# A chunked recurrence in one decoder trunk: three engines in a rewritten source order, the head norm in four stages, outputs in two tiles

## The chip, the cores and the metric

The kernel runs on 1 core of one Trainium2 chip. The metric is the device time of one execution in microseconds; a kernel's figure is the median of several runs. A run's time is a little longer than the span between its first and its last instruction in the trace.

## The reference, cut to what matters

The program is a two-layer decoder trunk over 512 tokens of width 1024: layer 0 is a sparse attention, layer 1 an RWKV-7 time mixing; each has a squared-ReLU MLP behind it. The change lies in the time mixing of layer 1, between the values and the output projection:

```python
def step(state, inp):
    r_t, w_t, k_t, v_t, kk_t, b_t = inp
    sa = jnp.einsum('bhvk,bhk->bhv', state, -kk_t)
    state = (state * w_t[:, :, None, :] + sa[..., None] * b_t[:, :, None, :]
             + v_t[..., None] * k_t[:, :, None, :])
    y = jnp.einsum('bhvk,bhk->bhv', state, r_t)
    return state, y
_, y = lax.scan(step, state0, (tm(rh), tm(wh), tm(kh), tm(vh), tm(kk), tm(bh)))
mean = jnp.mean(y, axis=-1, keepdims=True)
var = jnp.mean(jnp.square(y - mean), axis=-1, keepdims=True)
y = ((y - mean) * lax.rsqrt(var + LNX_EPS) * lnx_w + lnx_b)
bonus = jnp.sum(rh * kh * r_k, axis=-1, keepdims=True) * vh
out = (y + bonus).reshape(B, L, D) * g
return out @ w_o
```

There are 16 heads of 64 channels.

## The kernel before, in words

All of the time mixing stands in `rwkv()`. The scan over 512 tokens is done as 8 chunks of 64 tokens (NCH = 8). Within a chunk the recurrence is a triangular system: its 64x64 inverse is put together from two 32x32 diagonal inverses and an off-diagonal block. The diagonal inverses are made on VectorE by `invert()` and `solve()` (L999 to L1042) for four chunks at once: two halves, 0 for chunks 0 to 3 and 1 for chunks 4 to 7. One half is 30 pairs of a multiply (`pr`, L1025) and an add (`tn`, L1026) and a copy (L1029); then the tiles go to DRAM and back (`dm`, `dt`), to `T11` and `Mt`. `invert()` is a generator: `run(budget)` lets it go on by that many nanoseconds' worth of pairs, `until(f)` until half f is issued.

The values GEMM (L1203 to L1215) steps the generator with `run(RUNW)` in each of its 8 rounds. Its result is copied to `VT` by ScalarE (`vcopy`, L1223), and VectorE takes means over it (`vmean`, L1273). Before a chunk can start, its operands are made: `opl(n, j)` (j = 0, 1) has 32 small matmuls L1184/L1185 into a `d` bank, which VectorE masks into `abd` and `BL` (L1179, four instructions for each j); `opt(n)` (L1196) transposes eight blocks, copied out to `BL` (L1197, L1113 and, in part, L1111 on VectorE); `vload(n)` (L1280) adds the mean to v on GpSimd, into `sv`, and sends v to a `vb` tile with two DMAs. `merge1` (L1129) and `merge2` (L1139) make the off-diagonal block; between them stands a copy `sa`, behind them one into `Mt`.

A chunk's own chain on TensorE: `step_z` (L1308, z; reads `sv`, copied to `bd`), `step_u` (L1324, u; four copies L1113 into `sv`), `step_r` (L1317) and `step_y` (L1354) for the output, `step_s` (L1335) and `step_n` (L1342) for the next state, which VectorE scales into `sv` (L1346) and ScalarE copies into `bd` (L1348). So z of the next chunk waits for L1346. The output y is copied to a `y` tile (L1357).

`gnorm(n)` normalizes y over a head: square (ScalarE, L1378), sum (VectorE, L1379), root and two Newton steps (L234 to L239), scale (L1381), then on GpSimd the weight `lnw` (L1383), the bonus `bv` = `vb` times `bo` (L1386) and the sum (L1387). `turn(n)` (L1396) transposes y; `out(f)` (L1404) multiplies with the gate `gT` for the chunks of half f, and `wo(f)` (L1409) is the output projection, 8 groups of 24 matmuls of 128x256 over `oh`, `ol` and `w`, with high and low parts split on ScalarE (L93, L104), VectorE (L101) and GpSimd (L99). `g2` (L1244 to L1247, 8 groups of 4 matmuls of 128x512) makes the gate `gT`.

The order of the work: the loop over chunks stands in `manual_schedule` for TensorE alone, so TensorE runs in source order, and the scheduler places ScalarE's and VectorE's instructions by priorities. In the source the operands, the merge and the norm of neighbouring chunks are generators that are stepped between the three stages of a step; `fill()` puts `g2` groups (table G2P) and `wo(0)` groups (table WOP) at numbered places in between. `turn` stands two steps behind its chunk (TD = 2), `out(0)` in step 5, and four of the eight `wo(0)` groups in steps 6 and 7 (before y of chunk 7 is done), the other four behind it.

Of the kernel before, what the change touches and what calls it, by code (L numbers as in the profile page):

```python
# [765 lines left out]
def rwkv(c, x, ks, gi):  # L766
# [324 lines left out]
    bo = c.tmp.tile([128, NCH, 8], F32, name="bo", tag="bo", bufs=1)  # L1091
    for b in range(2):
        for s in range(2):
            nc.vector.tensor_copy(bo[E2[b], s::2].rearrange("p n (a e) -> p n a e", e=2), pbo[E2[s], :, :, b])
# [20 lines left out]
    def merge(n):  # L1115
        mt = Mt[n // 4][:, :, n % 4]
        t11 = T11[n // 4]
        with c.hp("merge"):
            sa = merge1(mt, t11, n)
        yield  # L1120
        with c.hp("merge"):
            merge2(mt, sa)
        yield

    def merge1(mt, t11, n):
# [9 lines left out]
    def merge2(mt, sa):  # L1135
# [57 lines left out]
    def opt(n):  # L1193
# [4 lines left out]
        for i in range(2):  # L1198
            cp(TE[i], BL[n][E2[1 - i], 1, :, 64:128], pt[E2[i], :, 1])
# [28 lines left out]
    for i in VL:  # L1228
        vcopy(i)
    del ps  # L1230
    SV, YY, gT = {}, {}, {}

    def g2():
        (ah, al), (bh, bl) = ((a.rearrange("p a b -> p (a b)") for a in c.wget(0)) for _ in range(2))
        nc.scalar.activation(bh[64:96], bl[64:96].bitcast(F32), AF.Copy)
        for m in range(KC):
            g2m(m, ah, al, bh)
            yield

    @c.site("g2")  # L1240
    def g2m(m, ah, al, bh):
# [4 lines left out]
        nc.tensor.matmul(p, al[:, ms], sg[0], start=False, stop=False)  # L1246
# [30 lines left out]
    def vload(n):  # L1277
# [4 lines left out]
        VB[n] = c.t("vb")  # L1282
        v4 = vt(n).rearrange("p (a b) e i -> p a b (e i)", b=2)
        for b in range(2):
            nc.sync.dma_start(VB[n][E2[b]].rearrange("p (a j) -> p a j", a=4), v4[:, :, b])

    w0 = None
    fill()
    vmean(0)
    vload(0)  # L1290
    for _ in opnd(1):
        fill()
    lnw = c.t("lnw").rearrange("p (q i) -> p q i", i=64)
    nc.sync.dma_start(lnw, c.aps["lnw"])
    bd = c.b8("bd", F32, (128, 2, 8, 2, 64))
    nc.gpsimd.memset(bd, 0.0)
    Zb, Sb = bd[:, 0], bd[:, 1]
    yT, o, xo = {}, {}, []

    @c.site("step_z")  # L1300
    def step_z(n):
        pz, py = c.bank("g", (128, 8, 64)), c.bank("g", (128, 4, 2, 64))
        if n == 0:
            for e in range(2):
                nc.gpsimd.memset(SV[n][E2[e], e], 0.0)
# [3 lines left out]
        cp(0, Zb[E2[0], :, 0], pz[E2[0]])  # L1309
        cp(ZE, Zb[E2[1], :, 1], pz[E2[1]])  # L1310
        return py

    @c.site("step_r")
    def step_r(n, py):
        if n:
            for q in range(8):
                nc.tensor.matmul(py[E2[q % 2], q // 2].rearrange("p a b -> p (a b)"), sl(AR, n, q)[:, 1],  # L1317
                                 Sb[:, q].rearrange("p a b -> p (a b)"), start=q < 2, stop=False, skip_group_check=True)

    @c.site("step_u")  # L1320
    def step_u(n):
# [4 lines left out]
        for b in range(2):  # L1326
            for e in range(2):
                cp(UE[2 * b + e], par(SV[n][:, e])[E2[e], :, b], pu[E2[b], :, e])
# [10 lines left out]
    def step_n(n, pn):  # L1339
# [11 lines left out]
    def step_y(n, py):  # L1351
# [265 lines left out]
```

## Time and profile before

| what | value |
|---|---|
| median of 3 runs | 1375.86 us (1373.76 to 1376.73) |
| the profiled execution | 1374.03 us |
| its span, first to last instruction | 1372.2 us |
| mean granted TensorE clock, share of full | 0.972 |
| busy: TensorE, VectorE, ScalarE, GpSimd | 94%, 58%, 43%, 12% of the span |
| last matmul of the values / first matmul of the MLP of layer 1 | 816.2 us / 1005.0 us |

The busy share of the whole span says little here: TensorE is full in the GEMMs around the recurrence. What the change touches is a stretch of some 170 us, and there the questions are which wait ends last at each step and which clock TensorE was granted. The profile gives the clock as a share: 1.00 is the full level (2.4 GHz), 0.50 the half level (1.2 GHz), and a stretch with 0.82 has had some of both.

### The profile page before, as it was taken

What the parts mean: (1) busy time and instruction counts of PE and PEld (TensorE: products, weight loads), DVE (VectorE), ACT (ScalarE), POOL (GpSimd) and SP (SyncE); (2) the same over time, 40 slices, a digit from 0 to 9 for tenths busy, and PEclk for the clock granted to TensorE, in tenths of its full rate; (3) what the DMA queues carried; (4) which work ended last, traced back from release to release, by engine and by line L of the source; (5) the groups of instructions that cost most, each with busy time, mean ns of one, the idle gap of its engine ahead of it and who ended that gap; (6) DMA issues with size and microseconds to landing.
All of it is one profiled execution on the core that took longest, in us unless ns stands there. A gap on an engine that the chain in (4) does not pass through costs nothing.

```text
span 1372.2 us, 20054 instructions
## 1 busy us (share of the span) xinstructions
PE 1295.9 (94%) x8197; PEld 1065.6 (78%) x8197; DVE 800.8 (58%) x1429; ACT 593.6 (43%) x1005; POOL 171.3 (12%) x168
## 2 busy tenths in 40 slices
PE   7989899999999999999999896877999999999997
PEld 6767566888888888898578674667988888888887
DVE  5689974553431445339888888577865532245422
ACT  5545693343311434228776332655543421134421
POOL 0386750000000000000000011334220000000000
PEclk9999999999999999999999895989999999999998
DMA  7100013221323224303302414433532222322401
GB/s 287 62 31 32 1 69 117 100 93 62 123 92 123 80 74 153 123 32 123 123 31 53 128 52 98 74 95 132 185 105 80 92 92 94 122 92 83 162 1 62
DMA packets 68283, 128.04 MB, mean 93 GB/s; under 512 B 32864, under 2 KB 39648, under 8 KB 67424
## 3 DMA queue, kind: packets, MB, share of 16 engines
q1 hardware_dynamic: 65952, 124.53, 27.7%
q10 hardware_dynamic: 2240, 2.24, 0.5%
q8 instruction: 64, 1.05, 0.3%
q14 instruction: 27, 0.22, 0.0%
HBM read 115.74 MB, written 6.82 MB: 89 GB/s over the span
## 4 chain that ended last, share of the span: by engine, by line
PE 80%; DVE 12%; issue 3%; ACT 2%; POOL 2%; DMA 1%; SPq 0%; ACTq 0%; DVEq 0%; POOLq 0%
PE g L119 20%; PE g L120 20%; PE g L121 20%; PE g L628 2%; PE d L613 1%; DVE rot L411 1%; DVE w L101 1%; DVE L L587 1%; DVE pr L1025 1%; DVE tn L1026 1%; POOL kl L99 1%; DVE acc L497 1%; PE g L1308 1%; PE g L993 1%; PE g L1324 1%
## 5 line engine op out<-in xcount | busy, mean ns | idle before, releaser
L101 DVE TENSOR_TENSOR w<-wraw,w 128x1024 fp32r<-128x1024 f32 x189 | 232.8, 1255 | 109.4 <-ACT w L93 109.1
L93 ACT ACTIVATE w<-wraw 128x1024 fp32r<-128x1024 f32 x198 | 201.2, 1048 | 139.9 <-DMA wraw<-in_wblk 106.9
L119 PE MATMUL g<-sh,w 128*128 128x512 f32 (+1 forms) x608 | 216.5, 356 | 0.0
L120 PE MATMUL g<-sl,w 128*128 128x512 f32 (+1 forms) x608 | 216.1, 355 | 0.0
L121 PE MATMUL g<-sh,w 128*128 128x512 f32 (+1 forms) x608 | 216.1, 355 | 0.0
L120 PE MATMUL g<-al,w 128*128 128x512 f32 x512 | 200.0, 391 | 0.2 <-DVE al L257 0.2
L119 PE MATMUL g<-ah,w 128*128 128x512 f32 x512 | 200.1, 391 | 0.0
L121 PE MATMUL g<-ah,w 128*128 128x512 f32 x512 | 199.9, 390 | 0.0
L273 ACT ACTIVATE sh<-r 128x512 fp32r<-128x512 f32 x64 | 40.4, 631 | 227.2 <-DVE r L271 227.2
L119 PEld LDWEIGHTS g<-sh,w 128*128 128x128 f32 x608 | 114.9, 189 | 16.4
L121 PEld LDWEIGHTS g<-sh,w 128*128 128x128 f32 x608 | 114.9, 189 | 16.3
L120 PEld LDWEIGHTS g<-sl,w 128*128 128x128 f32 x608 | 114.9, 189 | 16.2
L119 PEld LDWEIGHTS g<-ah,w 128*128 128x128 f32 x512 | 96.5, 189 | 20.2
L120 PEld LDWEIGHTS g<-al,w 128*128 128x128 f32 x512 | 96.4, 188 | 20.4 <-DVE al L257 0.6
L121 PEld LDWEIGHTS g<-ah,w 128*128 128x128 f32 x512 | 96.5, 189 | 20.1
L271 DVE SCALAR_TENSOR_TENSOR r<-g,rstd 128x512 f32<-128x512 f32 x64 | 44.1, 691 | 97.0 <-PE g L121 84.6
L275 DVE TENSOR_TENSOR sl<-q,sh 128x512 fp32r<-128x512 f32 x64 | 44.4, 693 | 75.1 <-ACT q L274 75.1
L295 DVE TENSOR_TENSOR x<-g,x 128x512 f32<-128x512 f32 x26 | 18.0, 691 | 107.4 <-PE g L121 107.4
L179 ACT ACTIVATE sq<-x 128x256 f32<-128x256 f32 (+1 forms) x56 | 26.7, 499 | 105.1 <-DVE x L295 56.4
L922 POOL MEMSET seg<- 128x512 f32 x1 | 0.5, 528 | 487.2 <-DVE xl L101 487.2
L597 ACT ACTIVATE L<-L,st 128x256 f32<-128x256 f32 (+3 forms) x64 | 35.1, 553 | 14.0 <-DVE st L595 13.9
L274 ACT ACTIVATE q<-r 128x512 f32<-128x512 f32 x64 | 39.4, 615 | 0.0
(310 smaller groups left out, 2458.6 us busy)
## 6 DMA issues: line engine op xcount, KB each, us to landing
wraw<-in_wblk SPq DMA_DIRECT2D x98, 1024.0 KB, 4.8
wraw<-in_wblk SPq DMA_DIRECT2D x5, 512.0 KB, 5.6
x<-in_xT SPq DMA_DIRECT2D x8, 256.0 KB, 5.1
x<-in_xT SPq DMA_DIRECT2D x2, 1024.0 KB, 6.5
xs<-x SPq DMA_DIRECT2D x2, 1024.0 KB, 4.9
abd<-AR SPq DMA_DIRECT2D x64, 32.0 KB, 1.9
vb<-VT SPq DMA_DIRECT2D x16, 128.0 KB, 3.8
x<-xs SPq DMA_DIRECT2D x2, 1024.0 KB, 5.1
```

The costliest lines, as they stand in the source:

```text
L93: s.wsp = s.nc.scalar.activation(hi, r, AF.Copy)
L101: s.nc.vector.tensor_sub(out, a, b)
L119: s.nc.tensor.matmul(p, whi[:, kc, :], ahi, start=first and kc == 0, stop=False)
L120: s.nc.tensor.matmul(p, whi[:, kc, :], alo, start=False, stop=False)
L121: s.nc.tensor.matmul(p, wlo[:, kc, :], ahi, start=False, stop=last and kc == KC - 1)
L179: nc.scalar.activation(sq, xk, AF.Square)
L271: nc.vector.scalar_tensor_tensor(r, p, 0.0, rstd, op0=OP.max, op1=OP.mult)
L273: nc.scalar.activation(hi, r, AF.Square)
L274: nc.scalar.activation(q, r, AF.Square)
L275: nc.vector.tensor_sub(lo, q, hi.bitcast(F32))
L597: nc.scalar.activation(L[g][:, :n], L[g][:, :n], AF.Exp, bias=nmx[:, g:g + 1], scale=0.125, accum_out=sm[:, g:g + 1])
L628: nc.tensor.matmul(po[HF[e]], v[sc // 2][:, j:j + 64], st8[tb, pr, e][:, sc], start=sc == 0, stop=sc == tb)
```

## The change

The loop over chunks becomes straight source order on three engines (`manual_schedule` for TensorE, ScalarE and VectorE), and all that the generators and `fill()` interleaved is written out:

- The inverse is finished first: `run(9e8)` and two `run(1)` stand ahead of the first `vcopy`. The later calls `run(RUN1)`, `run(RUN2)` remain in the source.
- All eight `g2` groups stand ahead of the first merge.
- A step n is z, `opl(n+1, 0)`, u, merge1 of chunk n+1, s, n, r, y, `opl(n+1, 1)`, merge2, opt, turn.
- `gnorm` is cut in four: `gA` (square), `gB` (sum), `gC` (root), `gD` (all the rest), placed in steps by the tables GA, GB, TU.
- `bo` is one copy; the bonus reads v straight from `VT`, so the 16 `vb` DMAs are gone. It is two GpSimd multiplies of 64 partitions instead of one of 128.
- y lies in two tiles of four chunks. The copies of z, u and sa are all on ScalarE.
- `out(0)`, the norms 6 and 7, turns 5 to 7 and all eight `wo(0)` groups stand behind the loop.

```diff
+    with c.tc.manual_schedule(engines=set(MAN)):
+        run(9e8)
+        run(1)
+        run(1)
+        for i in VL[:3]:
+            vcopy(i)
+        vmean(0)
+        vload(0)
+        opn(1, 0)
+        for i in VL[3:]:
+            vcopy(i)
+        opn(1, 1)
...
+        g2(0)
+        g2(1)
+        opt(1, (0, 0))
+        g2(2)
+        g2(3)
+        step_z(0)
+        for m in range(4, 8):
+            g2(m)
+        vload(1)
+        run(RUN1)
+        merge2(0, merge1(0))
+        for n in range(NCH):
...
+            if n:
+                step_z(n)
...
+            if n and more:
+                acopy(n + 1)
+                opn(n + 1, 0)
+                vload(n + 1)
+            for k in GB.get(n, ()):
+                gB(k)
...
+            step_u(n)
+            if more and n != 3:
+                sa[n + 1] = merge1(n + 1)
+            for k in GB.get(n, ()):
+                gC(k)
+            if more:
+                pn = step_s(n)
+                step_n(n, pn)
+            py = step_r(n)
+            if more:
+                sbd(n)
+            step_y(n, py)
+            for k in GB.get(n, ()):
+                gD(k)
...
+            if n and more:
+                opn(n + 1, 1)
+            if n == 3:
+                sa[4] = merge1(4)
+            if more:
+                merge2(n + 1, sa[n + 1])
+            if n and n < NCH - 2:
+                opt(n + 1, (0, 0) if n < 3 else TE)
+            for k in TU.get(n, ()):
+                turn(k)
+            for k in GA.get(n, ()):
+                gA(k)
+    c.prefetch(PFA)
+    out(0)
+    gB(6)
+    gC(6)
+    gD(6)
+    gA(7)
+    gB(7)
+    gC(7)
+    gD(7, nc.vector)
     w0 = wo(0)
...
+    turn(5)
+    turn(6)
+    for _ in w0:
+        pass
+    turn(7)
     out(1)
...
+MAN = (mybir.EngineType.PE, mybir.EngineType.Activation, mybir.EngineType.DVE)
+GA = {2: (0,), 3: (1, 2), 4: (3,), 5: (4,), 6: (5,), 7: (6,)}
+GB = {3: (0,), 4: (1, 2), 5: (3,), 6: (4,), 7: (5,)}
+TU = {4: (0,), 5: (1, 2), 6: (3,), 7: (4,)}
```

What this does to the order of an engine's instructions shows at three places. First VectorE around the end of the inverse's first half. Before, this stood there (L1179 are the masks of `opl(1, ...)`, L1273/L1274 is `vmean`, L1029 the copy that ends half 0):

```order
L1026 TENSOR_TENSOR tn<-tn,pr 128x5x26
L1179 TENSOR_TENSOR BL<-d,kon 128x4x64
L1025 TENSOR_TENSOR pr<-tn 128x108
L1179 TENSOR_TENSOR BL<-d,kon 128x4x64
L1026 TENSOR_TENSOR tn<-tn,pr 128x4x27
L1111 COPY BL<-d 64x8x64
L1025 TENSOR_TENSOR pr<-tn 128x84
L1274 TENSOR_SCALAR vm<-vm 128x16
L1273 TENSOR_REDUCE vm<-VT 128x16
```

Now the masks (L1171) and `vmean` (L1245) stand behind the last pair and the copy of half 1:

```order
L1025 TENSOR_TENSOR pr<-tn 128x30
L1026 TENSOR_TENSOR tn<-tn,pr 128x30
L1028 MEMSET tn 128x32
L1029 COPY tn<-tn 128x1024
L1245 TENSOR_REDUCE vm<-VT 128x16
L1246 TENSOR_SCALAR vm<-vm 128x16
L1171 TENSOR_TENSOR abd<-d,kon 64x4x64 x2
L1171 TENSOR_TENSOR BL<-d,kon 128x4x64 x2
L1171 TENSOR_TENSOR abd<-d,kon 64x4x64 x2
```

So `vmean`, the masks of chunk 1 and all that waits for them have moved from between the pairs of half 0 to behind the 30 pairs of half 1.

Second TensorE in step 6 before (L1342 is n, L1354 is y, L1396 a turn, L119 to L121 are `wo(0)`):

```order
L119 MATMUL g<-oh,w 128x256
L120 MATMUL g<-ol,w 128x256
L121 MATMUL g<-oh,w 128x256
L1342 MATMUL g<-sv,BL 64x64 x16
L1354 MATMUL g<-sv,BL 64x64 x16
L1396 MATMUL g<-ident,y 128x128 x4
```

And TensorE now from the end of step 6 on (L1131 is merge2, L1260 z, L1268 u, L1297 r, L1310 y, L1363 a turn):

```order
L1131 MATMUL g<-Mt,sa 32x32 x16
L1363 MATMUL g<-ident,y 128x128 x4
L1260 MATMUL g<-sv,abd 64x64 x16
L1268 MATMUL g<-bd,Mt 64x128 x8
L1297 MATMUL g<-bd,AR 64x128 x8
L1310 MATMUL g<-sv,BL 64x64 x16
L1363 MATMUL g<-ident,y 128x128 x12
L119 MATMUL g<-oh,w 128x256
L120 MATMUL g<-ol,w 128x256
```

The `wo(0)` matmuls have left the steps; the first of them stands behind three turns in a row, those of chunks 4, 5 and 6.

Third ScalarE at that place now (L1272 are the copies of u(7), L1315 y(7), L1364 a turn's copy, L1323 `gA`, L1335 `gC`, L93 and L104 high parts of `w` and of `ot`):

```order
L1272 ACTIVATE sv<-g 64x4x64 x4
L1335 ACTIVATE gst<-gst 128x8
L1315 ACTIVATE y<-g 128x512
L1364 ACTIVATE yT<-g 128x8x64
L1323 ACTIVATE sq<-y 128x512
L1364 ACTIVATE yT<-g 128x8x64
L1335 ACTIVATE gst<-gst 128x8
L93 ACTIVATE w<-wraw 128x1024 x4
L104 ACTIVATE oh<-ot 128x256 x6
L1323 ACTIVATE sq<-y 128x512
```

The norm of chunk 6 begins behind the copy of y(7), and the weights of `wo(0)` are split behind it; before, the first of these weights were split during steps 5 to 7.

## Rows read from the trace of the kernel before

**Rows 1.** Windows: length; busy PE, PEld, DVE, ACT, POOL; granted clock; DMA share, GB/s.
```profile
838.00:850.00 12.00, 7.83 (x112) 6.53 (x114) 10.99 (x32) 3.42 (x7) 0.00 (x0) 0.50 0.34 65
850.00:867.00 17.00, 16.79 (x372) 14.28 (x369) 10.59 (x30) 9.79 (x20) 3.32 (x4) 0.82 0.40 91
...
884.20:899.50 15.30, 11.42 (x274) 9.49 (x274) 9.09 (x19) 9.77 (x20) 5.03 (x5) 1.00 0.17 28
...
916.00:931.50 15.50, 12.10 (x271) 10.37 (x271) 13.33 (x24) 9.80 (x20) 5.78 (x5) 0.89 0.15 25
```

**Rows 2.** What TensorE waited for, 815 to 970 us: total us, times, longest.
```profile
PE g L1308 <- DVE sv L1346: 7.8, 7, 3.8
```

**Rows 3.** Timeline of TensorE, 815 to 854 us: start, us, instruction, idle before and releaser.
```profile
815.94 0.39 PE L1213 MATMUL g<-w,xh 128*128 128x512 f32 x1
816.16 0.39 PE L1214 MATMUL g<-w,xl 128*128 128x512 f32 x1
...
834.21 0.28 PE L1129 MATMUL g<-T,Mt 32*32 32x32 f32 x2 [9.04 <-DMA T<-dt]
...
851.61 2.40 PE L1342 MATMUL g<-sv,BL 128*64 128x64 f32 x31
```

**Rows 4.** VectorE by line, 810 to 828 us: count, busy us, mean ns, idle before.
```profile
L1273 DVE TENSOR_REDUCE vm<-VT 128x16 f32<-128x1024 f32 x4 | 4.8, 1212 | 3.3 <-ACT VT L1223 3.3
L1026 DVE TENSOR_TENSOR tn<-tn,pr 128x210 f32<-128x210 f32 (+9 forms) x10 | 2.8, 285 | 0.1
L1025 DVE TENSOR_TENSOR pr<-tn 128x198 f32<-128x198 f32 (+8 forms) x9 | 2.8, 316 | 0.2
...
L1179 DVE TENSOR_TENSOR BL<-d,kon 128x256 f32<-128x256 f32 x4 | 1.6, 409 | 0.0
```

**Rows 5.** VectorE by line, 828.8 to 851.6 us: all of half 1.
```profile
L1025 DVE TENSOR_TENSOR pr<-tn 128x30 f32<-128x30 f32 (+14 forms) x30 | 10.0, 332 | 1.0
L1026 DVE TENSOR_TENSOR tn<-tn,pr 128x30 f32<-128x30 f32 (+14 forms) x30 | 9.9, 331 | 1.0
L1029 DVE COPY tn<-tn 128x1024 f32<-128x1024 f32 x2 | 2.1, 1046 | 0.1
```

**Rows 6.** Timeline of ScalarE in chunk 3.
```profile
888.03 1.20 ACT L1113 ACTIVATE bd<-g 64x512 f32<-64x512 f32 x2
...
890.48 1.58 ACT L1113 ACTIVATE sv<-g 64x256 f32<-64x256 f32 x4 [0.47 <-PE g L1324]
893.86 0.63 ACT L1378 ACTIVATE sq<-y 128x512 f32<-128x512 f32 x1 [1.80 <-PE g L1139]
```

**Rows 7.** Timeline of TensorE, from z(7) to the first matmul of wo(1).
```profile
960.29 1.15 PE L1308 MATMUL g<-sv,abd 128*64 128x64 f32 x32
962.74 1.09 PE L1324 MATMUL g<-bd,Mt 128*64 128x128 f32 x16 [1.29 <-ACT bd L1113]
...
964.63 0.38 PE L119 MATMUL g<-oh,w 128*128 128x256 f32 x1
...
967.70 1.20 PE L1354 MATMUL g<-sv,BL 128*64 128x64 f32 x32
...
982.96 0.51 PE L119 MATMUL g<-oh,w 128*128 128x256 f32 x2
```

**Rows 8.** ScalarE and VectorE by line and form, 867 to 969 us: splitting w; scaling the state.
```profile
L93 ACT ACTIVATE w<-wraw 128x1024 fp32r<-128x1024 f32 x10 | 10.3, 1054 | 5.1 <-DMA wraw<-in_wblk 5.1
...
L1346 DVE TENSOR_TENSOR sv<-g,pc 64x512 f32<-64x512 f32 x11 | 7.6, 689 | 1.0 <-PE g L1342 0.7
```

**Rows 9.** Timeline of VectorE, 957 to 964 us: two low parts of w.
```profile
957.82 1.23 DVE L101 TENSOR_TENSOR w<-wraw,w 128x1024 fp32r<-128x1024 f32 x1 [0.84 <-ACT w L93]
...
961.13 2.24 DVE L101 TENSOR_TENSOR w<-wraw,w 128x1024 fp32r<-128x1024 f32 x1
```

**Rows 10.** Timeline of GpSimd, 938 to 965 us.
```profile
938.75 0.85 POOL L99 TENSOR_TENSOR ol<-ot,oh 128x256 fp32r<-128x256 f32 x1 [0.81 <-ACT oh L104]
...
961.02 1.26 POOL L1383 TENSOR_TENSOR y<-y,lnw 128x512 f32<-128x512 f32 x1 [6.18 <-DVE y L1381]
```

More of the change, by code (lines that the diff above doesn't have):

```diff
@@ L1113, in cp, with merge1 @@
             nc.scalar.activation(out, a, AF.Copy)
[L1115 to L1125, printed above, removed]
+    @c.site("merge")
+    def merge1(n):
+        mt, t11 = Mt[n // 4][:, :, n % 4], T11[n // 4]
         pa = c.bank("g", (128, 8, 64))[:, :, :32]
@@ L1133, in merge1, with merge2 @@
         return sa
-    def merge2(mt, sa):
+    @c.site("merge")
+    def merge2(n, sa):
+        mt = Mt[n // 4][:, :, n % 4]
         pm = c.bank("g", (128, 8, 64))[:, :, :32]
@@ L1308, in step_z @@
                 nc.tensor.matmul(pz[E2[e], q], AL[n][:, q, e], SV[n][:, e, q], start=True, stop=True)
[L1309 to L1318, printed above, removed]
+        for e in range(2):
+            nc.scalar.activation(Zb[E2[e], :, e], pz[E2[e]], AF.Copy)
     @c.site("step_u")
@@ L1346, in step_n, with step_r, sbd @@
             nc.vector.tensor_mul(SV[n + 1][E2[e], e], pn[E2[e]], pcb[E2[e]].to_broadcast([64, 8, 64]))
+    @c.site("step_r")
+    def step_r(n):
+        py = c.bank("g", (128, 4, 2, 64))
+        if n:
+            for q in range(8):
+                nc.tensor.matmul(py[E2[q % 2], q // 2].rearrange("p a b -> p (a b)"), sl(AR, n, q)[:, 1],
+                                 Sb[:, q].rearrange("p a b -> p (a b)"), start=q < 2, stop=False, skip_group_check=True)
+        return py
+    @c.site("step_r")
+    def sbd(n):
         for e in range(2):
@@ L1424, in wom @@
         nc.vector.tensor_add(xm, p, xm)
-    until(0)
-    w0 = wo(0)
-    for _ in merge(0):
-        fill()
-    with c.tc.manual_schedule(engines={mybir.EngineType.PE}):
-        for n in range(NCH):
-            if n == 3:
-                until(1)
-            s = step(n)
-            op, mg = iter(()), iter(())
-            if n + 1 < NCH:
-                if n % 2:
-                    vmean((n + 1) // 2)
-                vload(n + 1)
-                mg = merge(n + 1)
-                if n:
-                    op = opnd(n + 1)
-            for i in range(3):
-                next(s)
-                next(op, None)
-                if i < 2:
-                    next(mg, None)
-                if i == GN and n:
-                    gnorm(n - 1)
-                if i == TN and n >= TD:
-                    turn(n - TD)
-                    if n - TD == 3:
-                        out(0)
-                if 3 * n + i in PFS:
-                    c.prefetch(PFA)
-                if n < 3:
-                    run(RUN1)
-                fill()
@@ L1459, in rwkv, with opn @@
-    gnorm(NCH - 1)
-    for n in range(NCH - TD, NCH - 1):
-        turn(n)
-    pull(w0, 8)
-    turn(NCH - 1)
+    yT, o, xo, yq, sa = {}, {}, [], [], {}
+    def opn(n, j):
+        if j == 0:
+            BL[n] = c.b8("BL", F32, (128, 2, 8, 128))
+        opl(n, j)
+    with c.tc.manual_schedule(engines=set(MAN)):
[9 more added lines that the diff above has]
+            vcopy(i)
+        del ps
+        opn(1, 1)
+        (ah, al_), (bh, bl) = ((a.rearrange("p a b -> p (a b)") for a in c.wget(0)) for _ in range(2))
+        nc.scalar.activation(bh[64:96], bl[64:96].bitcast(F32), AF.Copy)
+        g2(0)
[10 more added lines that the diff above has]
+        for n in range(NCH):
+            more = n < NCH - 1
+            if n:
+                step_z(n)
+            if n % 2 and more:
+                vmean((n + 1) // 2)
+            if n == 1:
+                lnw = g3(c.t("lnw"))
+                nc.sync.dma_start(lnw, c.aps["lnw"])
+            if n and more:
[4 more added lines that the diff above has]
+                gB(k)
+            if n < 3:
+                run(RUN2)
+            step_u(n)
[12 more added lines that the diff above has]
+                gD(k)
+            if n < 2:
+                run(RUN2)
+            elif n == 2:
+                run(9e8)
+                run(1)
+                run(1)
+            if n and more:
[10 more added lines that the diff above has]
+                gA(k)
```

140 lines of the change are left out of this document (53 added, 87 removed).

## The prediction

> **What bounds the kernel now.** I read the windows first, then what TensorE waited for, then its timeline and that of the engines it waited for. Between the values GEMM and the first steps TensorE stands still or runs slowly: from 838 to 850 us it is busy 7.83 of 12 us at a granted clock of 0.50 (1.2 GHz), from 850 to 867 us it is full and the clock is 0.82 [rows 1]. The reader sees the cause in its timeline: behind the last value matmul at 816.2 it waits 9.04 us, up to 834.2, for the trip of the inverse through DRAM, and n(0) ends at 851.61 + 2.40 = 854.0 [rows 3]. In the loop a chunk is bound by hand-overs: from 884.2 to 899.5, 15.3 us at full clock, with one chunk in it and no other work, TensorE is busy 11.42, ScalarE 9.77, VectorE 9.09 [rows 1]; the wait that comes back in every chunk is that of z for the scaled state, 7.8 us over 7 times [rows 2]. Chunks with w splits beside them lose clock too (0.89 from 916 to 931.5) [rows 1]. In steps 6 and 7 `wo(0)` fills the gaps, so little is left behind y(7), which ends at 968.9; `wo(1)` starts at 982.96 [rows 7]. From there on both kernels do the same work, so I forecast when `wo(1)` starts.
>
> The sum is made against the profiled execution, 1374.0 us (span 1372.2 and 1.8 around it); the median of the runs, 1375.86, lies 1.8 above. A difference under 0.2%, about 2.7 us, can't be told from none here.
>
> **Part 1, the start: about 10 us later.** Ahead of `vmean` and the masks of chunk 1 VectorE now has the whole inverse. From 810.2 on: the rest of half 0, 2.8 + 2.8 us [rows 4], and a copy of 1.05 [rows 5], to 816.9. Half 1: 10.0 + 9.9 busy, 2.0 between them and a copy, 22.9 in all [rows 5], to 839.8. `vmean` 1.2 + 0.2 and four masks of 0.41 [rows 4]: 842.9. TensorE ends the values at 816.55 [rows 3] and has one half of `opl(1)` to do, about 1 us; the other half waits for the masks, since both `d` banks are taken. Everything in TensorE's source order stands behind it, g2 too. So it idles some 25 us, where it now idles in pieces.
>
> From 842.9 to the end of n(0), at full clock: half an `opl` 1.0; 8 g2 groups of 4 matmuls spaced 0.23 [rows 3], 7.3; opt 1.0; z 1.15, u 1.09 [rows 7]; n as long as z; the two merges 1.4 (my estimate from their 32 small matmuls each, under z's 32); the copies of sa and Mt, about 0.8 each, and of u, 1.58 [rows 6], in which TensorE waits; hand-overs 0.7. That is 18. Behind its idle time now, TensorE had 0.50 for 12 us and then 0.82 over 17 us, so about 6 us of those 17 at half [rows 1]; 6 us at half do 3 us of work, which puts n(0) at 864, against 854.0. Bounds: 861 (no clock loss) and 868 (half clock up to u). What covered the second half of the inverse before was TensorE's wait for the first; that cover is gone. The DMA trip of half 0 now lies inside the wait and costs nothing; that of half 1 is wanted only by chunk 4, some 40 us later. The `bo` copy, the memsets moved ahead and the 16 `vb` DMAs taken off SP's queue stand in nobody's wait: at nothing.
>
> **Part 2, the loop: about 27 us shorter.** A full chunk with norm and turn, from the end of n to the end of n. ScalarE sets the pace, since it is in order: scaled state 0.69 behind n [rows 8], its two copies and y 1.8, then what TensorE makes in the order r, y, opl, merge2 (3.9 behind n): Mt 0.8, two `BL` copies 1.2, the turn's copy 0.6, gA 0.63 [rows 6], which ends 7.4 behind n. z was ready at 6.75; its copies (1.20 [rows 6]) end at 8.6, u at 9.75, u's copies (1.58) at 11.3, n at 12.5. Without norm, turn and opt, n(1) follows in about 8.5; n(2) 11.4, n(3) 12.1; with two norms in a row and the late merge in it n(4) 14; n(5) and n(6) about 13.5 each. Sum 73. From n(6) to the end of y(7): scale 1.4, z 1.15, its copies 1.2, u 1.09, u's copies 1.58, y 1.2 [rows 6 to 8], with hand-overs 8. y(7) ends at 864 + 73 + 8 = 945. The clock: TensorE is busy nearly 11.4 of each 12.5, more than the 12.10 of 15.5 that had 0.89 [rows 1]; I take 4 to 8 us of loss, since there are gaps in each chunk, and y(7) at **951**, against 968.9 now. So the loop (from n(0)) takes 87 us, not 115. Of the 28 gained, four `wo(0)` groups (12) and the last g2 groups have only moved out.
>
> **Part 3, the tail: about 35 us longer.** Now 14.1 us lie between the end of y(7) and `wo(1)` [rows 7]. After: all eight `wo(0)` groups. One is 24 matmuls, 3.07 us from the first at 964.63 to y at 967.70 [rows 7]; eight: 24. But they cannot start at once. Both things they need begin behind y(7):
> - ScalarE, in order: copies of y, turn 4, square 6, turn 5, root 6, about 2.7; then four high parts of w at 1.05 [rows 8]: 6.9 behind y(7), and only then the high parts of the outputs.
> - VectorE, in order: norm 6 among eight products for the gate, about 8; then four low parts of w at 1.23, or 2.24 beside GpSimd [rows 9], 4.9 to 9.0; then a low part of an output. 13.3 to 17.5.
> - GpSimd, behind the norm's scaling at about 8: weight, low part, two bonus products, low part, sum, at 0.85 to 1.26 each [rows 10], 6.5 alone. turn(6), which stands ahead of the first `wo(0)` matmul, comes at 14.5, or 17 with delays.
>
> I take 16 us of idle time, midway, as both chains run beside each other. Behind it TensorE starts at half clock again, as at 838 [rows 1]: 3 us. `wo(0)` ends at 951 + 16 + 24 + 3 = 994. Then `wo(1)`: turn(7) has 23 matmuls (2.8 us) behind it as cover, but VectorE does eight products (3.5) and two w splits (2.5) before the first low part, and the copies ahead take 1.3: some 7.5 to 8 in a row, so a stall of 4 with bounds 0 and 6, and 1 for the clock. `wo(1)` starts at 999.5, against 982.96: **+16.5**, and 1374.0 + 16.5 is 1390.5; I say 1391.
>
> On the splits beside GpSimd the rows show 1.23 alone and 2.24 where GpSimd started an instruction 0.1 us earlier [rows 9, 10]. The Trainium skill ("SBUF — State Buffer", section Who interferes with whom) says that a VectorE instruction with two inputs in SBUF shares a port pair with GpSimd's reads, and that one of the two then blocks for the other's whole instruction. By that rule each of the four splits could wait out 1.26 us, 10.0 in all, and `wo(0)` would start 18 to 19 behind y(7), 1393; if GpSimd is the one that blocks, the turn is late instead. I keep 16, as the rows allow both 13 and 17.5.
>
> **The rivals.**
> 1. *The loop gains more than the tail loses: faster.* Place: ScalarE's queue in the loop. If its copies come early enough, TensorE paces a chunk with its own 11.2 (11.42 without the two starts of the next z [rows 1]) at full clock: n(6) at 864 + 8.5 + 5 x 11.2 = 928.5, y(7) at 936.5; the tail with the low ends (13 + 24 + 1.5 + 1) puts `wo(1)` at 976, 7 us earlier: 1367. It decides where y(7) ends before 943 with that tail, 12.5 for each of those five chunks. For it: ScalarE has under 9.8 of work per chunk [rows 1]; against: the square stands ahead of z's copies in its queue. With the tail as I forecast it, y(7) would have to end at 934.5, below that floor. 0.14.
> 2. *The two cancel:* y(7) at 943 to 946 with a tail of 39. 1372 to 1376. 0.07.
> 3. *The clock stays down:* the gaps of 1 to 2 us in each chunk and the idle 25 and 16 us keep it at about 0.8 over the loop and the start of `wo(0)`. 87 us with some 70 of TensorE work at 0.8 instead of 0.93: 10 to 12 more. 1402. For it: 0.82 over a window that was full [rows 1]; against: 1.00 in the chunk with 11.42 of 15.3 busy. 0.13.
> 4. *The change doesn't do what it says at the start:* the order of rows shows the inverse ahead, so only its price can be off. If VectorE does the pairs faster without interleaving (gaps of 2.0 gone), 2 us; this lies in the range.
>
> **How the numbers follow.** The forecast as told, 1383 to 1399, has 0.66. With rival 3 (0.13) slower cases hold 0.79; rival 2 0.07; rival 1 0.14. The range takes in the forecast, rival 2 and rival 3 up to 1402, leaving out rival 1 and the far end of 3: 1372 to 1402. Faster by over 0.2% 0.15, within 0.2% 0.07, slower 0.78.
>
> **What would show it.** Right: in the timeline of VectorE the masks of chunk 1 stand behind the copy of half 1 at about 841 to 843, and TensorE's longest wait, some 25 us, ends there with VectorE as releaser; n(0) ends near 864; z's follow each other in 12 to 14 us; y(7) near 951; then a second long wait of 13 to 18 us ending with a turn whose releaser is GpSimd's sum, or with the low part of `w`; clock near 0.5 behind both. Wrong: z's less than 11.5 apart from chunk 2 on, `wo(0)` starting under 10 us behind y(7), or TensorE at work between 820 and 840.

## The result, and the profile after

The changed kernel takes 1398.86 us, the median of 4 runs (1396.93 to 1400.9); the kernel before, in the same session, 1376.08 (1373.76 to 1376.73). The ratio is 1.0169, 95% interval 1.015 to 1.0188: **slower, by 22.8 us**, where +15 to +17 was forecast. It lies inside the range (1372 to 1402), near its upper end, and 0.1 us inside the 1383 to 1399 of the forecast as told. The profiled execution after has a span of 1397.7 us at a mean clock of 0.967, so 25.5 us more than the span of before; 2.0 of these stand ahead of the change already, since the values GEMM ends at 818.6 instead of 816.6.

What TensorE waited for, 815 to 1030 us after (total us, times, longest), four of the lines:

```profile
PE d L1176 <- DVE BL L1171: 25.0, 1, 25.0
...
PE g L1363 <- POOL y L1354: 19.3, 2, 16.2
...
PE g L1268 <- ACT bd L1262: 12.9, 7, 2.9
...
PE g L120 <- DVE ol L101: 4.5, 1, 4.5
```

The first line is the start (the second half of `opl(1)` for the masks), the second the tail (turns 5 and 6 for GpSimd's sum of the norm), the third the loop (u for the copies of z), the fourth the first low part of `wo(1)`. The wait of z for the scaled state [rows 2], 7.8 us before, is gone altogether.

The timeline of TensorE after, at the start and then from y(7) on (start, us, instruction, idle before and releaser), beside [rows 3, 7]:

```profile
844.57 0.44 PE L1176 MATMUL d<-AR,KB 64*64 64x128 f32 x1 [24.98 <-DVE BL L1171]
...
861.92 2.16 PE L1286 MATMUL g<-sv,BL 128*64 128x64 f32 x31
...
863.92 1.15 PE L1310 MATMUL g<-sv,BL 128*64 128x64 f32 x31
...
953.03 2.07 PE L1310 MATMUL g<-sv,BL 128*64 128x64 f32 x32
...
958.80 1.11 PE L1363 MATMUL g<-ident,y 128*128 128x128 f32 x4 [3.11 <-POOL y L1354]
...
976.10 1.12 PE L1363 MATMUL g<-ident,y 128*128 128x128 f32 x4 [16.18 <-POOL y L1354]
976.86 0.56 PE L119 MATMUL g<-oh,w 128*128 128x256 f32 x1
...
999.29 0.60 PE L1363 MATMUL g<-ident,y 128*128 128x128 f32 x4
...
1002.96 0.73 PE L119 MATMUL g<-oh,w 128*128 128x256 f32 x4 [0.32 <-ACT oh L104]
1008.22 0.58 PE L120 MATMUL g<-ol,w 128*128 128x256 f32 x1 [4.53 <-DVE ol L101]
```

n(0) ends at about 864, y(7) at 955.1, the first `wo(0)` matmul comes at 976.9, and `wo(1)` gets going at 1008.2 instead of 983. What ends the first wait is seen on VectorE, where the masks of chunk 1 come behind the copy of half 1 and `vmean`:

```profile
840.50 1.03 DVE L1029 COPY tn<-tn 128x1024 f32<-128x1024 f32 x1
...
842.90 0.86 DVE L1171 TENSOR_TENSOR abd<-d,kon 64x256 f32<-64x256 f32 x2
```

The windows after, beside [rows 1] (length; busy PE, PEld, DVE, ACT, POOL; clock; DMA share, GB/s):

```profile
838.00:850.00 12.00, 5.43 (x46) 4.53 (x47) 7.54 (x21) 1.05 (x2) 4.18 (x4) 0.56 0.40 98
850.00:867.00 17.00, 15.31 (x310) 12.52 (x312) 2.73 (x4) 12.34 (x26) 0.00 (x0) 1.00 0.21 33
900.00:917.00 17.00, 14.34 (x302) 11.80 (x303) 9.09 (x24) 9.26 (x22) 8.14 (x8) 0.80 0.11 18
...
960.00:980.00 20.00, 3.90 (x19) 3.91 (x20) 14.47 (x26) 10.46 (x20) 16.18 (x10) 0.50 0.37 141
```

In the last of these TensorE works 3.9 of 20 us, at the half level, while GpSimd is busy 16.18. That is the longest wait of the tail, and VectorE's and GpSimd's timelines show what stands in it:

```profile
963.16 4.62 DVE L101 TENSOR_TENSOR w<-wraw,w 128x1024 fp32r<-128x1024 f32 x4
967.71 1.09 DVE L101 TENSOR_TENSOR ol<-ot,oh 128x256 fp32r<-128x256 f32 x3
```

```profile
963.39 6.53 POOL L1353 TENSOR_TENSOR y<-y,lnw 128x512 f32<-128x512 f32 x1 [4.65 <-DVE y L1346]
969.88 0.90 POOL L99 TENSOR_TENSOR ol<-ot,oh 128x256 fp32r<-128x256 f32 x1
970.87 2.18 POOL L1351 TENSOR_TENSOR bv<-VT,bo 64x512 f32<-64x512 f32 x2
973.12 1.25 POOL L99 TENSOR_TENSOR ol<-ot,oh 128x256 fp32r<-128x256 f32 x1
974.34 1.70 POOL L1354 TENSOR_TENSOR y<-y,bv 128x512 f32<-128x512 f32 x1
```

The weight multiply of norm 6 takes 6.53 us where it took 1.26 [rows 10]. It begins 0.2 us behind the first of VectorE's four splits of w. These run undisturbed at 1.2 each, three low parts of outputs follow them without a gap, and the multiply ends 1.1 us behind the last of the seven, so it did nearly all of its 1.26 us of work behind them. All that turn(6) waits for queues behind it on GpSimd. In the kernel before the same two instructions met the other way round: the multiply began at 961.02, 0.1 us ahead of a split, took its 1.26, and the split took 2.24 instead of 1.23 [rows 9, 10].

### The profile page after: what moved, and what is told of

The parts are those of the page before. It is cut to its first block, busy times and chain, and to the rows that moved or that the text cites. A ratio compares the mean times of both kernels' runs of the same rounds, so it can differ in the third digit from the quotient of the medians.

```text
span 1397.7 us, 20048 instructions
## 1 busy us (share of the span) xinstructions
PE 1291.2 (92%) x8197; PEld 1061.7 (76%) x8197; DVE 793.3 (57%) x1407; ACT 601.2 (43%) x1024; POOL 182.9 (13%) x176
## 3 DMA queue, kind: packets, MB, share of 16 engines
q10 hardware_dynamic: 2240, 2.24, 0.5%
q8 instruction: 64, 1.05, 0.3%
## 4 chain that ended last, share of the span: by engine, by line
PE 81%; DVE 12%; ACT 3%; issue 2%; POOL 1%; DMA 0%; ACTq 0%; DVEq 0%; POOLq 0%
PE g L120 20%; PE g L119 20%; PE g L121 20%; PE g L628 2%; DVE w L101 1%; DVE rot L411 1%; DVE tn L1026 1%; DVE pr L1025 1%; PE d L613 1%; DVE acc L497 1%; DVE L L587 1%; DVE m L495 1%; PE g L1268 1%; PE g L1286 1%; ACT bd L1262 1%
## 5 line engine op out<-in xcount | busy, mean ns | idle before, releaser
L101 DVE TENSOR_TENSOR w<-wraw,w 128x1024 fp32r<-128x1024 f32 x189 | 229.0, 1238 | 108.7 <-ACT w L93 108.6
L93 ACT ACTIVATE w<-wraw 128x1024 fp32r<-128x1024 f32 x198 | 200.6, 1048 | 134.7 <-DMA wraw<-in_wblk 102.9
L119 PE MATMUL g<-sh,w 128*128 128x512 f32 (+1 forms) x608 | 216.5, 356 | 0.0
L121 PE MATMUL g<-sh,w 128*128 128x512 f32 (+1 forms) x608 | 216.1, 355 | 0.0
L119 PE MATMUL g<-ah,w 128*128 128x512 f32 x512 | 199.6, 390 | 0.0
L121 PE MATMUL g<-ah,w 128*128 128x512 f32 x512 | 199.2, 389 | 0.0
L119 PEld LDWEIGHTS g<-sh,w 128*128 128x128 f32 x608 | 114.9, 189 | 16.4
L121 PEld LDWEIGHTS g<-sh,w 128*128 128x128 f32 x608 | 114.9, 189 | 16.3
L120 PEld LDWEIGHTS g<-sl,w 128*128 128x128 f32 x608 | 114.9, 189 | 16.2
L121 PEld LDWEIGHTS g<-ah,w 128*128 128x128 f32 x512 | 96.1, 188 | 20.0
L119 PEld LDWEIGHTS g<-ah,w 128*128 128x128 f32 x512 | 96.1, 188 | 19.9
L120 PE MATMUL g<-ol,w 128*128 128x256 f32 x128 | 38.1, 299 | 4.5 <-DVE ol L101 4.5
L1176 PE MATMUL d<-AR,KB 64*64 64x128 f32 x256 | 18.7, 285 | 25.0 <-DVE BL L1171 25.0
```

What stands on the lines that cost most here:

```text
L93: s.wsp = s.nc.scalar.activation(hi, r, AF.Copy)
L101: s.nc.vector.tensor_sub(out, a, b)
L119: s.nc.tensor.matmul(p, whi[:, kc, :], ahi, start=first and kc == 0, stop=False)
L120: s.nc.tensor.matmul(p, whi[:, kc, :], alo, start=False, stop=False)
L121: s.nc.tensor.matmul(p, wlo[:, kc, :], ahi, start=False, stop=last and kc == KC - 1)
L1176: nc.tensor.matmul(pl[E2[1 - e], e, q].rearrange("p a t -> p (a t)"), k[:, 1], ar.rearrange("p a t -> p (a t)"), start=True, stop=True)
```

## The experiments

Each kernel is compared with the kernel before on the same chip, so what an edit is worth I take from the ratios: the changed kernel has 1.0169, and 0.001 is 1.4 us. Intervals are some 0.0025 to either side, so the difference of two ratios is known to some 3.5 to 5 us only: by time alone e1, e2, e3 and e4 can't be told from the changed kernel, and e13 hardly; there the traces have to carry the reading. Lines are numbered as in each kernel, up to seven away from one another. Positions in different traces differ through what comes ahead of the change (the values GEMM ends at 818.6 in the changed kernel and at 817.5 to 821.9 in the others), so I compare distances too, above all from the start of y(0) to that of y(7), "the loop": 113.9 us before, 89.1 after. e2 and e3 leave the loop as it is and have 88.0 and 89.6, e1 and e9 have 88.8 and 91.0; that is the scatter. Part of it is the clock: over the loop it was 0.94 on average in the changed kernel and in e2, and 0.91 in e9.

**1. The inverse interleaved again (e1, e9).**

```diff
-        run(9e8)
-        run(1)
-        run(1)
         for i in VL[:3]:
             vcopy(i)
```

> The changed kernel without the three calls that finish the inverse ahead of vmean; the later calls run(9000) and run(2500) then have pairs to place. My theory (the 30 pairs of half 1 on VectorE are what TensorE's 25.0 us wait for the masks consists of): that wait falls to under 5 us, n(0) ends near 842 instead of 864, and the kernel takes 1377 to 1383 us instead of 1399. Rival (the pairs are work that VectorE has to do somewhere before chunk 4, so the loop pays them back): n(0) earlier, but z(4) at most 8 us earlier, 1391 to 1396.

Measured: 1393.89 us, ratio 1.0151 (1.0125 to 1.0176). y(0) starts at 857.9 instead of 863.9, the loop keeps its 88.8 us. The time lies where the rival put it, but not for its reason: the pairs are not paid back in the loop. Of the 16 us or more that I expected at the start 6 came in the trace; the ratio has 2.5. TensorE's timeline and SP's queue show the new wait:

```profile
848.84 0.63 PE L1119 MATMUL g<-T,Mt 32*32 32x32 f32 x14 [3.65 <-DMA T<-dt]
```

```profile
840.18 6.04 SPq L1144 DMA_DIRECT2D abd<-AR  x8
846.26 0.59 SPq L1038 DMA_DIRECT2D T<-dt  x1
```

The last load of T of half 0 stands on SP's queue behind eight copies into `abd`, whose tile z(0) reads first. e9 changes the order of that queue on top of e1:

```diff
-'acopy': 400
+'acopy': -100
```

> The kernel of the first experiment (inverse not finished ahead of vmean) with the priority of the abd DMAs lowered from 400 to -100, so that on SP's queue the loads of T of half 0 stand ahead of the abd copies of chunk 2, which wait for z(0). My theory (there the gain at the start was cut by T: its last load stood behind eight abd DMAs until 846.3 and landed at 848.8): merge1(0) no longer waits for T, n(0) ends 4 to 6 us earlier than there (857.9), at 852 to 854, the kernel 1387 to 1390. Rival (merge1 waits for something else just as late, or the abd copies are now late for their own chunks): 1392 to 1396.

Measured: 1386.5 us, ratio 1.0099 (1.0072 to 1.0127); 9.6 us less than the change. The wait for T is gone. y(0) starts at 855.3, and in this trace, of the slowest of e9's four runs, the values GEMM ended 3.3 us later than in the changed kernel; from its end y(0) comes after 33.3 us, where it was 39.4 in e1 and 45.3 in the changed kernel. The priority was not changed alone, without the interleaving. Two waits remain at the start, 6.30 us for the masks and 3.53 for ScalarE, in TensorE's timeline of e9:

```profile
829.23 0.44 PE L1176 MATMUL d<-AR,KB 64*64 64x128 f32 x1 [6.30 <-DVE BL L1171]
...
836.32 0.79 PE L1236 MATMUL g<-sg,w 96*128 96x512 f32 x1 [3.53 <-ACT w L1411]
```

**2. TensorE's order behind the loop (e2).**

```diff
+    w0 = wo(0)
+    for _ in range(4):
+        next(w0)
     gB(6)
     gC(6)
     gD(6)
-    gA(7)
+    turn(5)
+    for _ in range(2):
+        next(w0)
+    turn(6)
...
```

> The changed kernel with TensorE's order behind the loop alone altered: six wo(0) groups ahead of turn(6), four of them ahead of turn(5); the other engines keep their order. My theory (turn(6) behind GpSimd's norm of chunk 6 holds wo(0) back): the first wo(0) matmul starts when the first low part of an output is there, 968 to 970 instead of 976.9, and the kernel takes 1389 to 1393. Rival (the weights' low parts on VectorE set the start anyway, or the turn's wait only moves behind the groups): 1397 to 1400.

Measured: 1398.08 us, ratio 1.0181 (1.016 to 1.0202): the rival, no gain. The first `wo(0)` matmul starts at 962.15, 8.4 us behind y(7) instead of 21.8, but then the groups wait for GpSimd's low parts, and run at the half level. TensorE and GpSimd of e2:

```profile
962.15 1.22 PE L119 MATMUL g<-oh,w 128*128 128x256 f32 x4 [7.81 <-ACT oh L104]
...
977.04 0.58 PE L120 MATMUL g<-ol,w 128*128 128x256 f32 x1 [3.57 <-POOL ol L99]
```

```profile
960.78 6.54 POOL L1353 TENSOR_TENSOR y<-y,lnw 128x512 f32<-128x512 f32 x1 [3.38 <-DVE y L1346]
967.28 0.90 POOL L99 TENSOR_TENSOR ol<-ot,oh 128x256 fp32r<-128x256 f32 x1
```

The multiply is as long as in the changed kernel, and the low parts stand behind it on the same queue. Only the thing that waits for GpSimd has changed. The clock was 0.50 from 957 to 980.

**3. Norm 6 off GpSimd (e3).**

```diff
-    gD(6)
+    gD(6, nc.vector)
     gA(7)
```

> The changed kernel with the weight multiply and the bonus sum of norm 6 on VectorE instead of GpSimd. My theory (the 6.53 us of GpSimd's weight multiply are 1.3 us of work and 5 us in which VectorE's four splits of w keep it out): turn(6) comes 9 to 11 us earlier, the first wo(0) matmul then waits for the low parts, near 969 to 971, and the kernel takes 1390 to 1394. Rival (GpSimd is slow there for another cause, and it is the bonus products or the low parts on GpSimd that are late): the sum on VectorE waits for them, 1396 to 1400.

Measured: 1394.49 us, ratio 1.0151 (1.0133 to 1.0169), 2.5 us less than the change, between the theory's range and the rival's. turn(6) comes 2.9 us sooner (idle 13.3 instead of 16.2), not 9 to 11. Now VectorE is the one held up, and GpSimd's bonus products as well:

```profile
963.80 6.00 DVE L101 TENSOR_TENSOR w<-wraw,w 128x1024 fp32r<-128x1024 f32 x4
```

```profile
966.82 3.89 POOL L1351 TENSOR_TENSOR bv<-VT,bo 64x512 f32<-64x512 f32 x2
```

The four splits take 6.00 instead of 4.62, the two products 3.89 instead of 2.18. So VectorE's splits meet whatever GpSimd does beside them; moving a norm's multiply away passes the cost on to other instructions of both engines.

**4. The squares behind z (e5).**

```diff
             if n:
                 step_z(n)
+                for k in GA.get(n - 1, ()):
+                    gA(k)
...
-            for k in GA.get(n, ()):
-                gA(k)
```

> The changed kernel with each norm's square (gA) placed behind the next step's z instead of ahead of it, so that ScalarE copies z first. My theory (ScalarE in order paces the later chunks, the square 0.63 us ahead of z's copies in each of six chunks): u follows z 0.6 us sooner, y(7) 3 to 4 us earlier, 1395 to 1396. Rival (GpSimd's and VectorE's waits pace the chunks from 3 on): under 1 us, 1398 to 1400.

Measured: 1387.85 us, ratio 1.0105 (1.0086 to 1.0124): 8.8 us less, more than twice what I expected. The loop is 83.4 instead of 89.1 us, and the wait for turn(6) 11.6 instead of 16.2. In the loop TensorE's wait for z's copies falls from 12.9 to 8.9 us, and the clock was 0.96 instead of 0.94, worth some 1.7. The second gain comes from the tail: norm 6 is far enough ahead now that its multiply misses the splits. GpSimd and VectorE of e5:

```profile
955.21 1.26 POOL L1353 TENSOR_TENSOR y<-y,lnw 128x512 f32<-128x512 f32 x1
```

```profile
958.02 4.63 DVE L101 TENSOR_TENSOR w<-wraw,w 128x1024 fp32r<-128x1024 f32 x4 [1.27 <-ACT w L93]
```

The multiply takes 1.26 us when it ends before the splits begin. With 6.53 behind their start and 1.26 clear of them, it is the overlap that costs 5 us, not the multiply.

**5. The weights split in the steps (e4).**

```diff
             for k in TU.get(n, ()):
                 turn(k)
+            if n > 2 and more:
+                c.prefetch(n - 2)
```

> The changed kernel with one weight of wo(0) split at the end of each of steps 3 to 6, instead of four in a row behind the loop. My theory (the four splits on VectorE in a row, 4.62 us, are what keeps GpSimd's weight multiply of norm 6 at 6.53 us, and that multiply ends the wait of turn(6)): the multiply takes about 1.3 us, turn(6) comes some 10 us sooner behind y(7) (at 11 instead of 21), the loop pays up to 4 us for 1.05 us more on ScalarE in four steps: 1390 to 1394. Rival (the cost is the norm's length, not the lock): turn(6) at 17 or later behind y(7), 1397 to 1402.

Measured: 1395.7 us, ratio 1.0168 (1.0139 to 1.0198): by the ratio no change. The loop pays 3.8 us (y(0) to y(7) 92.9): ScalarE has 1.05 us more in front of z's copies, and TensorE's wait for them grows from 12.9 to 16.5. In the tail the multiply takes 1.44, as expected, but the scheduler then puts four bonus products, those of norm 7 too, ahead of the sum that turn(6) waits for. GpSimd of e4:

```profile
967.88 1.44 POOL L1353 TENSOR_TENSOR y<-y,lnw 128x512 f32<-128x512 f32 x1
969.28 4.65 POOL L1351 TENSOR_TENSOR bv<-VT,bo 64x512 f32<-64x512 f32 x4
974.01 1.79 POOL L1354 TENSOR_TENSOR y<-y,bv 128x512 f32<-128x512 f32 x1
```

The wait falls from 16.2 to 12.7 only, and turn(6) comes 17.0 us behind y(7), as the rival had it. So the long multiply went with the splits, as the theory said, and GpSimd's own order is the next bound.

**6. Both copies of opt on ScalarE (e11).**

```diff
-                opt(n + 1, (0, 0) if n < 3 else TE)
+                opt(n + 1, (0, 0))
```

> The changed kernel with both copies of opt on ScalarE in every step; before, from step 3 on, one of them was on VectorE. My theory (with ScalarE in order its own copy stands behind VectorE's copy into the same BL tile, a wait of 1.7 us in each of three steps, and z's copies queue behind it): that wait goes, ScalarE pays 0.6 for the second copy, u follows z about 1 us sooner in chunks 4 to 6, 1394 to 1397. Rival (the steps from 3 on wait for something else): 1398 to 1401.

Measured: 1393.76 us, ratio 1.0132 (1.0107 to 1.0157), 5.1 us less; the loop is 82.5 instead of 89.1 us. Both copies read the same transposes and write into the same tile, and the trace has one waiting for the other. What e11 takes away is seen in ScalarE's timeline of the changed kernel, in step 4:

```profile
917.96 0.60 ACT L1189 ACTIVATE BL<-d 128x512 f32<-128x512 f32 x1 [0.25 <-PE d L1188]
922.01 0.59 ACT L1111 ACTIVATE BL<-d 64x512 f32<-64x512 f32 x1 [3.45 <-DVE BL L1109]
...
923.25 0.63 ACT L1323 ACTIVATE sq<-y 128x512 f32<-128x512 f32 x1
923.78 1.19 ACT L1262 ACTIVATE bd<-g 64x512 f32<-64x512 f32 x2
```

ScalarE's copy waits 3.45 us for VectorE's copy into the same tile (1.73 in step 5), and behind it the turn's copy, the square and at last z's copies wait, the ones that u needs. TensorE's wait for z's copies falls from 12.9 to 9.0 us. The rest of the loop's gain goes with the clock, 0.97 over the loop instead of 0.94, worth some 3 us; whether the shorter waits raised it is open. An instruction that was moved off ScalarE to spare it cost it more, because ScalarE is in order and has to wait for it.

**7. The bonus as before (e13).** v by 16 DMAs to `vb` tiles, four copies for `bo`, one multiply of 128 partitions:

```diff
-        for b in range(2):
-            nc.gpsimd.tensor_tensor(bv[E2[b]].rearrange("p (a e i) -> p a e i", a=4, e=2), v4[:, :, b],
-                                    bs[:, :, b, :, None].to_broadcast([64, 4, 2, 64]), op=OP.mult)
+        nc.gpsimd.tensor_mul(g3(bv), g3(VB.pop(n)), bo[:, n, :, None].to_broadcast([128, 8, 64]))
```

> The changed kernel with the bonus as before: v to vb tiles by 16 DMAs, one GpSimd multiply of 128 partitions instead of two of 64. My prediction put this part at nothing. If that holds: 1397 to 1400. Rival (two multiplies of 64 partitions take 2.15 us of GpSimd where one of 128 took 1.04, and in the tail norm 6 and the low parts queue on GpSimd): turn(6) 1 us sooner, 1396 to 1398. Third (the DMAs that the change took off SP's queue held T or the abd copies up): slower, 1400 to 1404.

Measured: 1393.25 us, ratio 1.014 (1.0117 to 1.0162): 4 us less, more than the 1 us of the rival, but at the edge of what the two intervals can tell from nothing. The price on GpSimd is as it said, one multiply in e13, and then two in the changed kernel, at the same place:

```profile
949.44 1.04 POOL L1355 TENSOR_TENSOR bv<-vb,bo 128x512 f32<-128x512 f32 x1
```

```profile
950.39 2.15 POOL L1351 TENSOR_TENSOR bv<-VT,bo 64x512 f32<-64x512 f32 x2
```

The wait for turn(6) falls by 1.9 us and that of `wo(1)` by 1.1. But this is not the changed kernel's tail with 1.1 us of GpSimd taken out. VectorE and GpSimd of e13:

```profile
961.87 6.76 DVE L101 TENSOR_TENSOR w<-wraw,w 128x1024 fp32r<-128x1024 f32 x4
```

```profile
962.09 2.12 POOL L1356 TENSOR_TENSOR y<-y,lnw 128x512 f32<-128x512 f32 x1 [4.15 <-DVE y L1353]
```

The multiply begins 0.2 us behind the first split, as in the changed kernel, and yet it takes 2.12 us and not 6.53: it gets its turn behind that split, and from there on the two engines take turns, so that the four splits need 6.76 us. Why they do so here and not there is open. So e13 shows the price of the two multiplies, and not how much of the time they are.

The loop is 85.5 instead of 89.1 us, and 2.9 of that lie between z(4) and y(4), where the changed kernel ran at the half level for a while and e13 did not. u(4) after takes 1.97 us, in e13 1.09:

```profile
906.73 1.97 PE L1268 MATMUL g<-bd,Mt 128*64 128x128 f32 x16 [2.33 <-ACT bd L1262]
```

```profile
909.62 1.09 PE L1275 MATMUL g<-bd,Mt 128*64 128x128 f32 x16 [2.32 <-ACT bd L1269]
```

TensorE waits as long ahead of u(4) in both. In e2, whose loop is that of the changed kernel, y(4) also comes as early as in e13 (9.0 us behind z(4), against 11.9; e2 ran at the half level later, from 919 to 926), so this piece can't be put down to the bonus; why the level fell at one place in one and not in the other is open.

**8. Several parts undone together (e7, e8, e12, e10).** e7 is e9, e5 and e4 in one:

> Together: the inverse not finished ahead, abd DMAs at low priority, the squares behind z, the weights of wo(0) split in steps 3 to 6. If the three costs are separate and add up (5 to 11 at the start, 11 for the squares, 5 to 8 for the weights): 1370 to 1377. Rival (all three end at one wait, that of the tail, and overlap): 1380 to 1388.

Measured: 1380.62 us, ratio 1.006 (1.0038 to 1.0083). The parts alone gave 9.6, 8.8 and 0.1 us, 18.5 together; here 15, which the intervals can't tell from 18.5. A reason for less would be that e5 and e4 both free the multiply of norm 6. The loop has not become shorter: 91.5 us, at a clock of 0.91. e8 adds TensorE's order of e2:

> The same together with TensorE's order of the second experiment, four wo(0) groups ahead of turn(5) and two more ahead of turn(6). My theory: with GpSimd free of the lock its low parts come in time, so the groups ahead of the turns now fill TensorE's wait for the norm: 5 to 9 us less than without, 1362 to 1371, and so the first version that beats the kernel before (1375). Rival (GpSimd still does the norm ahead of the low parts): no gain over the order without it.

Measured: 1381.11 us, ratio 1.0063 (1.0038 to 1.0089), no gain, the rival: with the multiply clear of the splits too, TensorE waits for GpSimd's low parts, which stand among the norm's work. e12 is e7 with opt's copies of e11:

> The kernel with three parts undone (inverse not finished ahead, abd DMAs at low priority, squares behind z, weights of wo(0) split in steps) and opt's copies on ScalarE. Theory: 2 to 4 us less than without the last part, 1377 to 1379, so still above the kernel before, because all of wo(0), 23 us of TensorE, stands behind y(7). Rival (opt's copy was hidden): 1380 to 1382.

Measured: 1376.11 us, ratio 1.0011 (0.9997 to 1.0026), as fast as the kernel before as far as 10 and 19 runs can tell, and by the ratio 6.7 us less than e7, where 2 to 4 was expected. So undoing these parts brings back nearly all that the change cost. Its loop is 85.5 us against 91.5 in e7 and 113.9 before, and the tail takes back what it gains: the first `wo(0)` matmul comes 16.0 us behind y(7), and all eight groups stand there. e10 puts three groups of `wo(0)` into step 7, as the kernel before had four in steps 6 and 7:

```diff
+            if n == 7:
+                out(0)
+                w0 = wo(0)
+                next(w0)
...
             step_u(n)
+            if n == 6:
+                turn(3)
+            if n == 7:
+                next(w0)
+                next(w0)
```

> The same with turn(3) right behind u(6), out(0) and three wo(0) groups in step 7 ahead of y(7), one behind it, two ahead of each of turn(5) and turn(6). Theory (the tail is long because wo(0) no longer fills TensorE's waits in the steps and for the norms): TensorE's waits behind z(7) fall from some 20 us to under 10, 1365 to 1372, faster than before. Rival (the outputs' splits now stand ahead of u(7)'s copies on ScalarE and delay the chain by as much): 1376 to 1382.

Measured: 1376.05 us, ratio 1.0016 (1.0001 to 1.0031). The rival. y(7) starts at 962.4 instead of 940.4. Ahead of it TensorE waits for ScalarE and GpSimd, most of the last two lines of its waits, and works at the half level from 940 to 957; behind it it waits for norm 6, the first line:

```profile
PE g L1363 <- POOL y L1354: 5.9, 1, 5.9
PE g L120 <- POOL ol L99: 4.5, 4, 3.8
PE g L119 <- ACT oh L104: 3.7, 2, 3.2
```

No version here beats the kernel before.

## Why the prediction was right, and where its sizes were off

**Part 1, the start, held.** TensorE waits 25.0 us for the masks, where 25 was said; VectorE's masks follow the copy of half 1 as forecast, and n(0) ends at 864. That this is the very figure is in part luck: the values GEMM ended 2.0 us later than in the trace of before, and the half level behind the wait lasted some 4 us (the clock is 0.64 from 844.5 to 850), where 6 was taken. e9 shows the cause: with the pairs out of the way, and T ahead of the `abd` copies, 9.6 us come back, 12 in its trace. It also shows a cost that only comes up without the pairs: SP's queue. Once the inverse is interleaved, the order of two groups of DMAs on it is worth 6 us at y(0), 7 by the ratios (e1 against e9). In the changed kernel the loads of half 0 stand on that queue by 824.4 us and the `abd` copies come at 852.7, so there it cost nothing, as forecast.

**Part 2, the loop, was right in kind and a little off in size.** y(7) was to end at 951 and did at 955.1. Up to z(4) the z's follow each other in 11.4 to 13.7 us, near the 12 to 14 that was said, two of them at the 11.5 that would have spoken against it; from then on in 16.1, 15.9 and 14.3. From the end of one n to the next it was 8.6, 11.4 and 12.1 us up to n(3), as forecast to 0.1 us; then 17.1, 15.6 and 15.6, where "n(4) 14; n(5) and n(6) about 13.5" stood, and 10.6 from n(6) to the end of y(7), where 8 stood. The 4 to 8 us for the clock cover a part of that: 0.94 over the loop is some 5 us. A term that was missing is ScalarE's wait of 3.45 and 1.73 us for VectorE's copy of opt into the same tile (e11). The queue of ScalarE that I named as the pace is confirmed by e5 and e4, by TensorE's wait for z's copies: 12.9 us falls to 8.9 with the squares, 0.63 us in each step, out of their way, and grows to 16.5 with 1.05 us of weights put in their way.

**Part 3, the tail, holds the largest error.** I took 16 us of idle time behind y(7), with bounds 13 and 17.5, and turn(6) at 14.5, or 17 with delays. TensorE idled 19.3 us, turn(6) came 21.0 and the first `wo(0)` matmul 21.8 us behind y(7). The term that was mis-sized is that of the splits of w beside GpSimd: "4.9 to 9.0" for VectorE, and 6.5 for GpSimd "alone". VectorE took 4.62, the low end; GpSimd bore it all, with 6.53 for one multiply. The rule of the Trainium skill that I cited ("SBUF — State Buffer", section Who interferes with whom: an instruction of one engine blocks the other) holds in so far as one engine stood still here; but GpSimd was not kept out for one instruction, it was for a run of seven, 963.39 to about 968.8. I had written that "if GpSimd is the one that blocks, the turn is late instead" without pricing it. With the 5.3 us that the multiply took over its 1.26 put on the 14.5, turn(6) comes to about 20. Eight groups and the clock took some 25.5 us, where 27 was said; the stall of `wo(1)` was 4.5 and 0.3 us and some behind it at half level, where 4 and 1 was said. The terms as written add up to 999, half a us less than the 999.5 that was told.

In all the tail was 4.6 us longer than forecast and the loop 4, so `wo(1)` got going 8.7 us later than the 999.5. Both errors went the same way, and the range held because it reached 11 us above the sum.

A part that the sum left out had a price: two multiplies of 64 partitions cost GpSimd 1.1 us more than one of 128 in each chunk (e13), and in the tail they stand on GpSimd between the multiply of norm 6 and the sum that turn(6) waits for. How much of the 22.8 us they are no run shows alone.

**The rivals.** The first (the loop gains more than the tail loses) failed where it said: the square and opt's copy stand ahead of z's copies, and y(7) did not come before 943. That rules out the second as well, which needed it at 943 to 946. The third (the clock stays down) was half there: 0.80 from 900 to 917 and 0.50 from 960 to 980, but 1.00 from 850 to 867. The fourth had no price left: the order and the 25.0 us came as forecast.

## What to carry to other kernels

Ask of every engine that becomes in order what else stands in front of the one instruction that the next engine waits for; a short instruction there (a square of 0.63 us, a copy that was given to another engine and now has to be waited for) costs its time in every round, and more where it tips the next meeting of two engines. When a run of back-to-back VectorE instructions with two operands in SBUF is moved next to GpSimd's work, price it in every way that the runs here showed: GpSimd stands still for the whole run, VectorE stands still for one instruction, or both take turns and both are late. And work that fills waits in a loop, moved behind it, is only free if nothing in the loop's last round (norms, splits, turns) has to be done before it.

## What the runs showed of the hardware that I had not expected

GpSimd can be left without a turn between VectorE instructions in a row: one multiply of 128x512 that began 0.2 us behind the first of seven took 6.53 or 6.54 us in five kernels (the changed one, e1, e2, e9, e11), 1.26 to 1.44 where the splits were out of its way (e5, e4). It need not be: in e13 it began just as far behind the first split and took 2.12, and VectorE's four splits 6.76. In e3, where GpSimd's instructions began otherwise, both lost: 6.00 instead of 4.62 and 3.89 instead of 2.18. What decides between these is open. On GpSimd a multiply of 64 partitions takes as long as one of 128 with the same elements in each (2.15 for two, 1.04 for one). The clock of TensorE after the wait of 25 us was 0.64 from 844.5 to 850 and 1.00 from there on; after the wait of 16 us it was 0.50 up to 980 and 0.96 from 980 to 1000.
